# Attention scores on all 128 array rows: q of one head with zeros in the other head's rows, three products against k of both heads

## The chip, the cores and the metric

One Trainium2 chip, one of its cores, one launch. The metric is the device time of the program in microseconds (us): the median of three runs was 327.04 us (326.93 to 328.31).

## What is computed

A layer of a decoder for one sequence of 256 tokens and 1024 channels: norm, causal attention with 16 heads of 64, output projection, residual, norm, a feed-forward with a causal convolution of width 3 over its 2 x 2816 inner channels, residual, last norm. Since the sequence has only 256 tokens and the blocks of the reference's block-sparse attention are 256 long, the block choice falls away and plain causal attention is left:

```
hn = rmsnorm(x) * norm_mix;  q, k, v = split(hn @ w_qkv)          # 16 heads of 64
s = (q / 8) @ k.T;  s = where(k_pos <= q_pos, s, -1e30);  p = softmax(s)
x = x + (p @ v) @ w_o
hn = rmsnorm(x) * norm_ffn;  u = conv3(hn @ ffn_w_up) + b;  gate, up = split(u)
x = x + (silu(gate) * up) @ ffn_w_down
out = rmsnorm(x) * norm_final
```

All of it is in 32-bit floats. The kernel gets near to that precision by splitting each operand into a high and a low part of the type fp32r and adding three products: high x high, high x low, low x high (`mm3`, L213 to L217: line L215 is high x high, L216 and L217 the other two).

## The kernel before, in words

Everything stays in SBUF but the weights, which stream in: a unit of weights is loaded by SP's queue, ScalarE (ACT) writes its high part (L158), VectorE (DVE) its low part (L161).

The heads go in pairs: pair j holds heads 2j and 2j+1, the first in partitions 0 to 63, the second in 64 to 127. For each pair TensorE (PE) makes qT and kT (128 channels x 256 tokens each, 24 products of 256 columns per projection, all with 128 x 128 weights); then the scores; ACT and DVE make the softmax; PE transposes the probabilities (L331) and multiplies them with V.

The queries are taken in two tiles of 128. The first 128 queries see only the first 128 keys, the second 128 see all 256. The steps that the change touches, per pair:

- `q_hi` (L259, ACT) and `q_lo` (L266, DVE) take q out of PSUM. For the first 128 queries q is copied as plain 32-bit floats (QF). For the second 128 a tile QS holds, for each head, the high part in that head's own 64 partitions and the low part in the other 64.
- `k_hi` (L274, ACT) writes, for each head, a tile KH with the high part of that head's k twice, in its own 64 partitions and in the other 64: four copies. `k_lo` (L281, DVE) writes the low part KL in two pieces of 64 partitions.
- `scores` (L286, PE): for each head one plain 32-bit product of 128 columns on 64 rows (L289); then for each head a product of QS with KH on all 128 rows (L291), which is q_hi k_hi + q_lo k_hi, and q_hi k_lo on 64 rows (L292). The profile's records show two records for each plain 32-bit product, so L289 has four per pair.
- `softmax_dve` (L297, DVE, L303) reads the scores with mask and takes the maxima.

What sets the order: a table written out by hand. `START` and `LAST` are the steps before and after the steady part; `SCHED` is one "tick", in which PE runs a projection of pair j, the transposes of pair j-2, the scores of pair j-1, the second projection, and P V. Every engine runs its own instructions in the order of this table; nothing is reordered by a scheduler. In a tick `OL`, `KH`, `QL`, `H0`, `KL` (the low part of the attention's output, the splits of k and q, and of the next weights) come first, then PE's `A`, `TR`, `SC`, ... DVE thus has OL, QL, KL in this order ahead of the scores. Loads are issued when a weight buffer comes free, which is when the low part of the unit in it is written.

After the eight pairs come the output projection, the residual and its transposes, and the feed-forward, eleven steps of two "up" projections and one "down" (L627 on). The gains of the last norm, gF, are loaded at L601 from ACT's queue.

Of the kernel before, what the change touches and what calls it, by code (L numbers as in the profile page):

```python
# [27 lines left out]
# The order in which the steps of the attention are issued; every engine runs its own in this order.  # L28
# Steps: Q, K, V = evacuation of a projection, H / L = high and low part of a split, SC = scores, MX = mask and
# maximum, E = exp, RC / N = normalisation, TR = transposes, T = split of the transposed, PV = times V, O = split  # L30
# of the output, A / B = projections, W = output projection. START: before the ticks, SCHED: a tick (steps marked 1
# belong to the tick before), LAST: after them ("-": left over from the last tick).
# [18 lines left out]
def hybrid_layer(ctx: ExitStack, tc: tile.TileContext, a):  # L51
# [40 lines left out]
    gF = cst.tile([P, D], F32, name="gF")  # L92
# [10 lines left out]
    # the activation tables, too, are loaded meanwhile  # L103
    act.activation(st[:, 31:32], neghalf[:, 0:1], AF.Exp)

    # PE clock warm-up while the first loads are under way
# [124 lines left out]
    # sum of squares -> 1/rms  # L231
# [7 lines left out]
    def bcast_R(c, alloc):  # L239
        # R[p, t] = st[t, c + t // 128] on all partitions  # L240
        rp = alloc()
        for t in range(2):
            dg = wk.tile([P, P], F32, name="dg")
            dve.tensor_scalar(dg, ident, st[:, c + t:c + t + 1], None, op0=ALU.mult)
            pe.matmul(rp[:, t * P:(t + 1) * P], ones, dg, start=True, stop=True)
        act.activation(R, rp[:, :S], AF.Copy)

    # ================= attention =================
# [5 lines left out]
    QF, QS, KF, KH, KL = {}, {}, {}, {}, {}  # L254
    rows = [slice(0, 64), slice(64, P)]

    # The second 128 queries' scores: a head's q_hi and q_lo lie one above the other (the second head's
    # lo above its hi) against k_hi twice, which is q_hi k_hi + q_lo k_hi in one pass; then q_hi k_lo.
    def q_hi(j):  # L259
        QF[j] = wk.tile([P, S], F32, name="QF", tag="y1")  # L260
        QS[j] = wk.tile([P, 2, P], F32R, name="QS", tag="y0")
        for h in range(2):
            act.activation(QS[j][rows[h], h, :], qps[j][rows[h], P:S], AF.Copy)
        act.activation(QF[j][:, 0:P], qps[j][:, 0:P], AF.Copy)

    def q_lo(j):  # L266
        for h in range(2):
            dve.tensor_sub(QS[j][rows[1 - h], h, :], qps[j][rows[h], P:S], f32(QS[j][rows[h], h, :]))
# [5 lines left out]
    def k_hi(j):  # L274
        KH[j] = [wk.tile([P, S], F32R, name=f"KH{h}", tag=("mh", "ml")[h], bufs=3) for h in range(2)]
        for h in range(2):
            act.activation(KH[j][h][rows[h], :], KF[j][rows[h], :], AF.Copy)
        for h in range(2):
            act.activation(KH[j][h][rows[1 - h], :], KF[j][rows[h], :], AF.Copy)

    def k_lo(j):  # L281
        KL[j] = wk.tile([P, S], F32R, name="KL", tag="KT")
        for h in range(2):
            dve.tensor_sub(KL[j][rows[h], :], KF[j][rows[h], :], f32(KH[j][h][rows[h], :]))

    def scores(j):  # L286
        SP[j] = [psS(0), psS(1)]
        for h in range(2):
            pe.matmul(SP[j][h][:, 0:P], QF[j][rows[h], 0:P], KF[j][rows[h], 0:P], start=True, stop=True)  # L289
        for h in range(2):  # L290
            pe.matmul(SP[j][h][:, P:P + S], QS[j][:, h, :], KH[j][h], start=True, stop=False)  # L291
            pe.matmul(SP[j][h][:, P:P + S], QS[j][rows[h], h, :], KL[j][rows[h], :], start=False, stop=True)  # L292
# [483 lines left out]
```

## Time and profile before

| | |
|---|---|
| median of three runs (lowest, highest) | 327.04 us (326.93, 328.31) |
| the profiled execution, span from first to last instruction | 325.3 us |
| PE busy | 313.4 us (96%), 2087 products |
| DVE busy | 244.9 us (75%) |
| ACT busy | 211.5 us (65%) |
| mean granted clock of TensorE | 0.993 |

The profiled execution is known by its span; what lies around it is the difference to a run's time, 1.7 us against the median. A product's busy time in the profile is longer than the distance to the next one, since products overlap: the pace is read from start to start.

### The profile page before, as it was taken

To read this page: it belongs to the slowest core of one execution; us is meant where nothing else is said; L and a number is where in the kernel's file an instruction comes from. 1 tells how busy PE (TensorE), PEld (TensorE's weight loads), DVE (VectorE), ACT (ScalarE), POOL (GpSimd) and SP (SyncE) were. 2 spreads that over 40 slices of the span, in tenths; PEclk is the share of its full clock that TensorE was granted. 3 is DMA by queue.
4 is the path that set the end of the run, shared out by engine and by line. 5 is a ranking of instruction groups with operands and counts; after the bars stand their busy time and mean duration, and the time that the engine had idled before them with its cause. 6 is when DMAs were issued, how large, how long until landed. Compare 5 with 4: busy or idle time off the path is not lost.

```text
span 325.3 us, 5446 instructions
## 1 busy us (share of the span) xinstructions
PE 313.4 (96%) x2087; PEld 283.3 (87%) x2087; DVE 244.9 (75%) x478; ACT 211.5 (65%) x397; POOL 4.7 (1%) x17
## 2 busy tenths in 40 slices
PE   8799999999999999999999999999999999999990
PEld 5688988887987888999999999999999999999970
DVE  3764898877898985489998777777777777774754
ACT  5775999877998954577776555556555565553342
POOL 1000000000000000000000000000000000000002
PEclk9999999999999999999999999999999999999997
DMA  6998333844123197418765555555555512110003
GB/s 168 379 413 345 133 129 131 322 148 176 66 82 114 43 351 317 141 55 319 287 236 195 193 196 193 195 193 192 178 183 175 184 61 64 66 64 2 1 1 129
DMA packets 12698, 55.50 MB, mean 171 GB/s; under 512 B 1408, under 2 KB 2304, under 8 KB 8960
## 3 DMA queue, kind: packets, MB, share of 16 engines
q1 hardware_dynamic: 12384, 54.37, 46.2%
q10 hardware_dynamic: 288, 0.79, 0.7%
q8 instruction: 16, 0.26, 0.3%
q14 instruction: 10, 0.08, 0.1%
HBM read 54.10 MB, written 1.05 MB: 170 GB/s over the span
## 4 chain that ended last, share of the span: by engine, by line
PE 93%; DMA 2%; SPq 1%; issue 1%; ACT 1%; DVE 1%; POOLq 0%; POOL 0%
PE psA L215 21%; PE psA L217 21%; PE psA L216 20%; PE psT L217 4%; PE psT L216 4%; PE psT L215 4%; PE psS L216 3%; PE psS L217 3%; PE psS L215 3%; DMA raw<-in_wqk 2%; PE psT L331 2%; PE psS L291 2%; PE psS L292 2%; PE psS L289 1%; PE psA L406 1%
## 5 line engine op out<-in xcount | busy, mean ns | idle before, releaser
L215 PE MATMUL psA<-XTh,whi 128*128 128x256 f32 x288 | 81.8, 284 | 0.0
L217 PE MATMUL psA<-XTh,wlo 128*128 128x256 f32 x288 | 81.7, 284 | 0.0
L216 PE MATMUL psA<-XTl,whi 128*128 128x256 f32 x288 | 81.4, 283 | 0.0
L161 DVE TENSOR_TENSOR wlo<-raw,whi 128x1024 fp32r<-128x1024 f32 (+2 forms) x52 | 56.6, 1094 | 9.1 <-ACT whi L158 8.9
L215 PEld LDWEIGHTS psA<-XTh,whi 128*128 128x128 f32 x288 | 54.4, 189 | 1.2
L610 ACT ACTIVATE y<-pad,head 128x256 f32<-128x256 f32 x44 | 25.9, 600 | 44.4 <-DVE pad L606 44.4
L216 PEld LDWEIGHTS psA<-XTl,whi 128*128 128x128 f32 x288 | 54.2, 188 | 0.4
L217 PEld LDWEIGHTS psA<-XTh,wlo 128*128 128x128 f32 x288 | 54.3, 189 | 0.0
L158 ACT ACTIVATE whi<-raw 128x1024 fp32r<-128x1024 f32 (+2 forms) x52 | 48.6, 950 | 4.2 <-DMA raw<-in_wqk 2.7
L606 DVE TENSOR_TENSOR pad<-psA,R 128x256 f32<-128x256 f32 x44 | 18.1, 420 | 38.2 <-PE psA L217 35.5
L615 DVE SCALAR_TENSOR_TENSOR y<-pad,head,y 128x256 f32<-128x256 f32 x88 | 37.0, 478 | 1.6 <-ACT y L610 1.5
L161 DVE TENSOR_TENSOR dlo<-rawd,dhi 128x1024 fp32r<-128x1024 f32 x29 | 35.3, 1216 | 0.2
L158 ACT ACTIVATE dhi<-rawd 128x1024 fp32r<-128x1024 f32 x29 | 30.2, 1048 | 2.2 <-PE psA L217 2.1
L217 PE MATMUL psA<-XTh,OTl 128*128 128x256 f32 x80 | 22.8, 285 | 0.0
L217 PE MATMUL psA<-XTh,Vl 128*128 128x256 f32 x80 | 22.7, 284 | 0.0
L216 PE MATMUL psA<-XTl,OTh 128*128 128x256 f32 x80 | 22.7, 284 | 0.0
L216 PE MATMUL psA<-XTl,Vh 128*128 128x256 f32 x80 | 22.7, 283 | 0.0
L215 PE MATMUL psA<-XTh,Vh 128*128 128x256 f32 x80 | 22.5, 281 | 0.0
L215 PE MATMUL psA<-XTh,OTh 128*128 128x256 f32 x80 | 22.5, 281 | 0.0
L657 ACT ACTIVATE sact<-y 128x256 f32<-128x256 f32 x22 | 9.2, 418 | 16.4 <-DVE y L615 16.4
L217 PE MATMUL psT<-dhi,ml 128*128 128x512 f32 x42 | 16.7, 396 | 0.0
L216 PE MATMUL psT<-dlo,mh 128*128 128x512 f32 x42 | 16.6, 395 | 0.0
(169 smaller groups left out, 663.2 us busy)
## 6 DMA issues: line engine op xcount, KB each, us to landing
raw<-in_wup SPq DMA_DIRECT2D x22, 1024.0 KB, 4.8
rawd<-in_wdn SPq DMA_DIRECT2D x22, 512.0 KB, 3.5
raw<-in_wqk SPq DMA_DIRECT2D x5, 1024.0 KB, 9.3
rawd<-in_wo SPq DMA_DIRECT2D x8, 512.0 KB, 3.9
raw<-in_wv SPq DMA_DIRECT2D x4, 512.0 KB, 6.7
raw<-in_wv SPq DMA_DIRECT2D x2, 1024.0 KB, 4.7
raw<-in_wqk SPq DMA_DIRECT2D x6, 256.0 KB, 6.3
x_sb<-in_x SPq DMA_DIRECT2D x2, 512.0 KB, 9.3
```

Of the source, the lines that this page charges most:

```text
L158: act.activation(self.hi[:, c], self.raw[:, c], AF.Copy)
L161: dve.tensor_sub(self.lo[:, c], self.raw[:, c], f32(self.hi[:, c]))
L215: pe.matmul(out, lh, rh, start=first, stop=False)
L216: pe.matmul(out, lh, rl, start=False, stop=False)
L217: pe.matmul(out, ll, rh, start=False, stop=last)
L291: pe.matmul(SP[j][h][:, P:P + S], QS[j][:, h, :], KH[j][h], start=True, stop=False)
L292: pe.matmul(SP[j][h][:, P:P + S], QS[j][rows[h], h, :], KL[j][rows[h], :], start=False, stop=True)
L331: pe.transpose(PT[j][:, h, b * P:(b + 1) * P], PR[j][:, h, b * P:(b + 1) * P], ident)
L606: dve.tensor_mul(pads[c % 2][g][:, 2:S + 2], gps[c, g][:, :S], R)
L610: act.activation(y[c, g], pads[c % 2][g][:, 2:S + 2], AF.Identity, scale=cw[:, 2, g * NC + c:g * NC + c + 1], bias=cb[:, g * NC + c:g * NC ...
L615: dve.scalar_tensor_tensor(y[c, g], pads[c % 2][g][:, j:j + S], cw[:, j, col:col + 1], y[c, g], op0=ALU.mult, op1=ALU.add)
L657: act.activation(sact, y[c, 0], AF.Silu)
```

## The change

q is kept in four constant tiles, QMh and QMl (high and low), two of each for odd and even pairs, 128 x 2 x 256. For head h only its own 64 partitions are ever written by `q_hi` and `q_lo`; the other 64 are set to zero once, by eight memsets on POOL at the start. k is split like any other operand: one high tile of 128 x 256, one low tile, with both heads in it. The scores are `mm3` on all 128 rows for each head and each tile of queries: the rows of the other head meet zeros. That is 12 products per pair, six of 128 columns (first queries) and six of 256 columns, in the place of two plain 32-bit ones and four fp32r ones.

To make room, gF is no longer a constant tile but two halves that take the buffers of the probabilities (tag PR), loaded in two transfers at the same place; the small diagonal tile of `bcast_R` takes the buffer y0.

```
+    QMh = [cst.tile([P, 2, S], F32R, name=f"QMh{i}") for i in range(2)]
+    QMl = [cst.tile([P, 2, S], F32R, name=f"QMl{i}") for i in range(2)]
+    for i in range(2):
+        for t in (QMh[i], QMl[i]):
+            pool.memset(f32(t[64:P, 0, :]), 0.0)
+            pool.memset(f32(t[0:64, 1, :]), 0.0)
...
     def q_hi(j):
-        QF[j] = wk.tile([P, S], F32, name="QF", tag="y1")
-        QS[j] = wk.tile([P, 2, P], F32R, name="QS", tag="y0")
         for h in range(2):
-            act.activation(QS[j][rows[h], h, :], qps[j][rows[h], P:S], AF.Copy)
-        act.activation(QF[j][:, 0:P], qps[j][:, 0:P], AF.Copy)
+            act.activation(QMh[j % 2][rows[h], h, :], qps[j][rows[h], :S], AF.Copy)
 
     def q_lo(j):
         for h in range(2):
-            dve.tensor_sub(QS[j][rows[1 - h], h, :], qps[j][rows[h], P:S], f32(QS[j][rows[h], h, :]))
+            dve.tensor_sub(QMl[j % 2][rows[h], h, :], qps[j][rows[h], :S], f32(QMh[j % 2][rows[h], h, :]))
...
     def k_hi(j):
-        KH[j] = [wk.tile([P, S], F32R, name=f"KH{h}", tag=("mh", "ml")[h], bufs=3) for h in range(2)]
-        for h in range(2):
-            act.activation(KH[j][h][rows[h], :], KF[j][rows[h], :], AF.Copy)
-        for h in range(2):
-            act.activation(KH[j][h][rows[1 - h], :], KF[j][rows[h], :], AF.Copy)
+        KH[j] = wk.tile([P, S], F32R, name="KH", tag="mh", bufs=3)
+        act.activation(KH[j], KF[j], AF.Copy)
 
     def k_lo(j):
-        KL[j] = wk.tile([P, S], F32R, name="KL", tag="KT")
-        for h in range(2):
-            dve.tensor_sub(KL[j][rows[h], :], KF[j][rows[h], :], f32(KH[j][h][rows[h], :]))
+        KL[j] = wk.tile([P, S], F32R, name="KL", tag="ml", bufs=3)
+        dve.tensor_sub(KL[j], KF[j], f32(KH[j]))
 
     def scores(j):
         SP[j] = [psS(0), psS(1)]
+        qh, ql = QMh[j % 2], QMl[j % 2]
         for h in range(2):
-            pe.matmul(SP[j][h][:, 0:P], QF[j][rows[h], 0:P], KF[j][rows[h], 0:P], start=True, stop=True)
-        for h in range(2):
-            pe.matmul(SP[j][h][:, P:P + S], QS[j][:, h, :], KH[j][h], start=True, stop=False)
-            pe.matmul(SP[j][h][:, P:P + S], QS[j][rows[h], h, :], KL[j][rows[h], :], start=False, stop=True)
+            for t in range(2):
+                q, n = slice(t * P, (t + 1) * P), (t + 1) * P
+                o = SP[j][h][:, 0:P] if t == 0 else SP[j][h][:, P:P + S]
+                mm3(o, (qh[:, h, q], ql[:, h, q]), (KH[j][:, :n], KL[j][:, :n]), True, True)
...
-    nc.scalar.dma_start(gF, bass.AP(tensor=a["gF"].tensor, offset=a["gF"].offset, ap=[[0, P], [1, D]]))
+    gF = [wk.tile([P, 512], F32, name=f"gF{i}", tag="PR") for i in range(2)]
+    for i in range(2):
+        nc.scalar.dma_start(gF[i], bass.AP(tensor=a["gF"].tensor, offset=a["gF"].offset + 512 * i, ap=[[0, P], [1, 512]]))
```

On PE, the scores of a pair in the steady part; psS are the two score tiles, one per head (left out<-moving operand, stationary operand, with the size of the output). Before:

```order
L289 MATMUL psS_655<-KF,QF 128x128
L289 MATMUL psS_656<-KF,QF 128x128
L291 MATMUL psS_655<-KH_607,QS 128x256
L292 MATMUL psS_655<-KL,QS 128x256
L291 MATMUL psS_656<-KH_608,QS 128x256
L292 MATMUL psS_656<-KL,QS 128x256
```

With the change (L222 to L224 are now the three lines of `mm3`):

```order
L222 MATMUL psS_651<-KH,QMh_90 128x128
L223 MATMUL psS_651<-KL,QMh_90 128x128
L224 MATMUL psS_651<-KH,QMl_92 128x128
L222 MATMUL psS_651<-KH,QMh_90 128x256
L223 MATMUL psS_651<-KL,QMh_90 128x256
L224 MATMUL psS_651<-KH,QMl_92 128x256
L222 MATMUL psS_652<-KH,QMh_90 128x128
L223 MATMUL psS_652<-KL,QMh_90 128x128
L224 MATMUL psS_652<-KH,QMl_92 128x128
L222 MATMUL psS_652<-KH,QMh_90 128x256
L223 MATMUL psS_652<-KL,QMh_90 128x256
L224 MATMUL psS_652<-KH,QMl_92 128x256
```

Six products became twelve, head by head, and k's low part (KL) is read by the second product instead of the fourth.

On DVE, between two softmaxes of the steady part (OTl is the low part of the attention's output, QS and QM that of q, KL that of k, wlo that of the next weights). Before:

```order
L272 TENSOR_TENSOR KF<-psA,R 128x256
L325 TENSOR_SCALAR PR<-PR,sm 128x256 x2
L359 TENSOR_TENSOR OTl<-psA,OTh 64x256 x2
L268 TENSOR_TENSOR QS<-psA,QS 64x128 x2
L284 TENSOR_TENSOR KL<-KF,KH_607 64x256
L284 TENSOR_TENSOR KL<-KF,KH_608 64x256
L161 TENSOR_TENSOR wlo<-raw,whi 128x1024
```

With the change:

```order
L275 TENSOR_TENSOR KF<-psA,R 128x256
L325 TENSOR_SCALAR PR<-PR,sm 128x256 x2
L359 TENSOR_TENSOR OTl<-psA,OTh 64x256 x2
L271 TENSOR_TENSOR QMl_93<-psA,QMh_91 64x256 x2
L283 TENSOR_TENSOR KL<-KF,KH 128x256
L168 TENSOR_TENSOR wlo<-raw,whi 128x1024
```

The places are the same; q's low part is twice as wide, k's is one instruction instead of two.

## Rows read from the trace of the kernel before

**Rows 1.** The page: the span, and each engine's busy time.
```profile
span 325.3 us, 5446 instructions
PE 313.4 (96%) x2087; PEld 283.3 (87%) x2087; DVE 244.9 (75%) x478; ACT 211.5 (65%) x397; POOL 4.7 (1%) x17
```

**Rows 2.** The chain that ended last, by line, shares of the span.
```profile
PE psA L215 21%; PE psA L217 21%; PE psA L216 20%; PE psT L217 4%; PE psT L216 4%; PE psT L215 4%; PE psS L216 3%; PE psS L217 3%; PE psS L215 3%; DMA raw<-in_wqk 2%; PE psT L331 2%; PE psS L291 2%; PE psS L292 2%; PE psS L289 1%; PE psA L406 1%
```

**Rows 3.** Timeline of PE, scores of pair 0: start, duration (us), engine, line, operands.
```profile
33.22 0.28 PE L215 MATMUL psA<-XTh,whi 128*128 128x256 f32 x1
...
34.16 0.28 PE L217 MATMUL psA<-XTh,wlo 128*128 128x256 f32 x1
34.38 0.49 PE L289 MATMUL psS<-KF,QF 64*128 64x128 f32 x4
34.80 0.39 PE L291 MATMUL psS<-KH,QS 128*128 128x256 f32 x1
35.11 0.38 PE L292 MATMUL psS<-KL,QS 64*128 64x256 f32 x1
...
36.05 0.39 PE L215 MATMUL psA<-XTh,whi 128*128 128x256 f32 x1
36.27 0.27 PE L216 MATMUL psA<-XTl,whi 128*128 128x256 f32 x1
```

**Rows 4.** Timeline of PE's weight loads, same stretch.
```profile
33.46 0.19 PEld L215 LDWEIGHTS psA<-XTh,whi 128*128 128x128 f32 x1
...
35.11 0.18 PEld L292 LDWEIGHTS psS<-KL,QS 64*128 64x128 f32 x1
```

**Rows 5.** Timeline of PE, scores of pair 1, first record and second one behind them.
```profile
42.59 0.49 PE L289 MATMUL psS<-KF,QF 64*128 64x128 f32 x4
...
44.49 0.28 PE L216 MATMUL psA<-XTl,whi 128*128 128x256 f32 x1
```

**Rows 6.** The chain in order of time: start, length, what.
```profile
28.29 0.45 PE psS L245 x4
...
42.01 0.66 PE psT L331 x6
```

**Rows 7.** Timeline of PE before the scores of pair 4: products of 512 columns.
```profile
71.71 0.40 PE L215 MATMUL psA<-whi,XTh 128*128 128x512 f32 x1
71.94 0.39 PE L216 MATMUL psA<-wlo,XTh 128*128 128x512 f32 x1
...
73.15 0.49 PE L289 MATMUL psS<-KF,QF 64*128 64x128 f32 x4
```

**Rows 8.** Groups by line and form, ACT, DVE and POOL: busy us, mean ns.
```profile
L279 ACT ACTIVATE KH<-KF 64x256 fp32r<-64x256 f32 x16 | 6.7, 417 | 0.4
L665 ACT ACTIVATE mh<-m 128x256 fp32r<-128x256 f32 x22 | 9.2, 418 | 11.3 <-DVE m L662 11.3
L284 DVE TENSOR_TENSOR KL<-KF,KH 64x256 fp32r<-64x256 f32 x16 | 6.7, 419 | 0.5
L668 DVE TENSOR_TENSOR ml<-m,mh 128x256 fp32r<-128x256 f32 x22 | 9.2, 418 | 1.5 <-ACT mh L665 1.5
L268 DVE TENSOR_TENSOR QS<-psA,QS 64x128 fp32r<-64x128 f32 x16 | 4.6, 289 | 1.7 <-ACT QF L264 1.4
L359 DVE TENSOR_TENSOR OTl<-psA,OTh 64x256 fp32r<-64x256 f32 x12 | 5.0, 420 | 1.4 <-ACT OTh L354 1.2
L82 POOL MEMSET mask<- 128x256 f32 x1 | 0.3, 312 | 0.0
```

**Rows 9.** Timeline of DVE before the scores of pair 0.
```profile
30.78 0.59 DVE L268 TENSOR_TENSOR QS<-psA,QS 64x128 fp32r<-64x128 f32 x2
...
32.91 1.41 DVE L376 SCALAR_TENSOR_TENSOR Vl<-psT,st,Vh 128x512 fp32r<-128x512 f32 x2
34.24 0.86 DVE L284 TENSOR_TENSOR KL<-KF,KH 64x256 fp32r<-64x256 f32 x2
```

**Rows 10.** Timeline of DVE before the scores of pair 4.
```profile
71.20 0.85 DVE L359 TENSOR_TENSOR OTl<-psA,OTh 64x256 fp32r<-64x256 f32 x2
72.06 0.59 DVE L268 TENSOR_TENSOR QS<-psA,QS 64x128 fp32r<-64x128 f32 x2
```

**Rows 11.** Windows: stretch, length, then busy us (count) of PE, PEld, DVE, ACT, POOL; clock, DMA.
```profile
51.93:61.20 9.27, 9.27 (x70) 8.34 (x70) 7.93 (x21) 8.29 (x23) 0.00 (x0) 1.00 0.34 123
...
140.00:313.00 173.00, 173.00 (x1217) 162.50 (x1217) 133.39 (x232) 99.71 (x146) 0.00 (x0) 1.00 0.42 150
```

More of the change, by code (lines that the diff above doesn't have):

```diff
@@ L90, in hybrid_layer @@
             pool.memset(pads[i][g][:, 0:2], 0.0)
-    gF = cst.tile([P, D], F32, name="gF")
+    QMh = [cst.tile([P, 2, S], F32R, name=f"QMh{i}") for i in range(2)]
[4 more added lines that the diff above has]
+            pool.memset(f32(t[0:64, 1, :]), 0.0)
     x_sb = cst.tile([P, 2, D], F32, name="x_sb")
@@ L242, in bcast_R @@
         for t in range(2):
-            dg = wk.tile([P, P], F32, name="dg")
+            dg = wk.tile([P, P], F32, name="dg", tag="y0")
             dve.tensor_scalar(dg, ident, st[:, c + t:c + t + 1], None, op0=ALU.mult)
@@ L253, in hybrid_layer @@
     qps, kps, SP, PR, PT, OP = {}, {}, {}, {}, {}, {}
-    QF, QS, KF, KH, KL = {}, {}, {}, {}, {}
+    KF, KH, KL = {}, {}, {}
     rows = [slice(0, 64), slice(64, P)]
     def q_hi(j):
-        QF[j] = wk.tile([P, S], F32, name="QF", tag="y1")
-        QS[j] = wk.tile([P, 2, P], F32R, name="QS", tag="y0")
         for h in range(2):
-            act.activation(QS[j][rows[h], h, :], qps[j][rows[h], P:S], AF.Copy)
-        act.activation(QF[j][:, 0:P], qps[j][:, 0:P], AF.Copy)
+            act.activation(QMh[j % 2][rows[h], h, :], qps[j][rows[h], :S], AF.Copy)
     def q_lo(j):
         for h in range(2):
-            dve.tensor_sub(QS[j][rows[1 - h], h, :], qps[j][rows[h], P:S], f32(QS[j][rows[h], h, :]))
+            dve.tensor_sub(QMl[j % 2][rows[h], h, :], qps[j][rows[h], :S], f32(QMh[j % 2][rows[h], h, :]))
     def k_evac(j):
@@ L693, in gains @@
         hs = slice(512 * half, 512 * half + 512)
-        dve.tensor_mul(x_sb[:, t, hs], x1[:, t, hs], gF[:, hs])
+        dve.tensor_mul(x_sb[:, t, hs], x1[:, t, hs], gF[half])
     def scaled(t, half):
@@ L734, in hybrid_layer @@
             nc.scalar.dma_start(a["out"][P:, :512], x_sb[:, 1, :512])
-        dve.scalar_tensor_tensor(x_sb[:, t, 512:], x1[:, t, 512:], st[:, 14 + t:15 + t], gF[:, 512:],
+        dve.scalar_tensor_tensor(x_sb[:, t, 512:], x1[:, t, 512:], st[:, 14 + t:15 + t], gF[1],
                                  op0=ALU.mult, op1=ALU.mult)
```

## The prediction

> **What bounds the kernel now.** I read the busy times first: TensorE (PE) is busy in 313.4 of 325.3 us, DVE in 244.9, ACT in 211.5 [rows 1]. That alone is a weak sign, since a busy PE may be a slow one, so the chain of waits comes next: it lies on PE almost throughout, and what other engines add is the load of the first weights at the start and the last norm at the end [rows 2]. The windows say the same by stage: in a tick of the attention PE fills 9.27 of 9.27 us while DVE has 7.93 and ACT 8.29, and in the feed-forward it fills 173.00 of 173.00 [rows 11]. So a microsecond taken from PE between 20 and 313 us comes off the end, as long as ACT and DVE keep up; work taken from ACT or DVE alone is worth nothing.
>
> Then I read PE's pace, from start to start. Nine projection products of 256 columns begin at 33.22 and the ninth at 34.16: 0.94 us / 8 = 0.118 us each [rows 3]. The score block beside them has another pace: the four L289 records take 0.42 us, and then L291 to L292 takes 0.31, though L291 has the same 256 columns and the same 128 rows as a projection. The loads tell why: in the projections the load of 0.19 us lies under earlier products (one every 0.118 us); in the block the load of L292 starts at 35.11, with its own product [rows 3, 4]. Where a product on 128 rows follows one on 64 rows or the other way round, nothing is loaded ahead. The first projection behind the block pays it too: 36.05 to 36.27 is 0.22 instead of 0.118.
>
> **The change, part by part.**
>
> *What goes.* For pair 1 the block runs from 42.59 to the second projection product behind it at 44.49: 1.90 us, less 0.118 for the projection between = 1.78 us [rows 5]. The blocks of the other pairs look alike. Pair 0 begins 0.22 us behind the last projection, so it has 0.10 us of switch in front as well [rows 3].
>
> *What comes.* Twelve products on 128 rows, in one mode with all their neighbours, so I take no switch. Six have 256 columns: 6 x 0.118 = 0.708 us. Six have 128 columns in fp32r, and **no row shows such a product**. Bounds: below, the step from 512 columns (71.71 to 71.94, 0.23 us [rows 7]) to 256 (0.118) is proportional, which would make 128 columns 0.06. Above, a plain 32-bit product of 128 columns on 128 rows, L245: four records in 0.45 us are two products, 0.225 each [rows 6]. Between them stand the transposes, 128 columns on 128 rows with a 128 x 128 load each, six in 0.66 us = 0.110 [rows 6]. I take 0.110: it is the nearest in shape, and a load of 0.19 us has to be fitted in for every product, which is already paced at 0.118 for twice the columns. Block: 0.708 + 0.66 = 1.37 us; it saves 1.78 - 1.37 = 0.41 us.
>
> The Trainium skill ("TensorE: Matmul & The Clock Gate", Back-to-back issue gap) gives about 81 ns per product for a stream of loads and products of 128 columns. By it the block would take 1.19 us and the sum would end near 323.0 us; no run here shows that pace for 32-bit operands.
>
> The same page (Part 3) has a rule against this change: a weight load overlaps products in flight only when it goes to another row group. This trace differs: in the projections all rows are the same and the load does overlap [rows 3, 4].
>
> *k's low part is read earlier.* Before, the fourth product needed it, now the second. Pair 0: DVE runs without a gap from 30.78 [rows 9]; the two low parts of q grow from 0.59 to about 0.85 (2 x 64x128 at 289 ns become 2 x 64x256 like L359 at 420 [rows 8]), so KL starts at 34.24 + 0.26 = 34.50 and, as one instruction of 0.42 [L668 in rows 8], ends at 34.92. The second product could start at 34.28 + 0.11 = 34.39 and waits 0.53. Eleven products follow, 5 x 0.110 + 6 x 0.118 = 1.26, up to 36.18. The old block ended, with its delayed projection, at 36.27 - 0.118 = 36.15. **Pair 0 gains nothing.** Pair 4: the low part of the output ends at 72.05 [rows 10], + 0.85 + 0.42 = 73.32; the second product would start at 73.15 + 0.11 = 73.26 [rows 7] and waits 0.06: gain 0.35. For the other six I take no wait: each tick DVE has 2 x (420 - 289) more for q and 2 x 419 - 418 less for k, 0.16 us less in all, and ACT four copies of k fewer (two of 417 ns as L279, two like them) for one of 418: 1.25 us less [rows 8]; its copies of q go from three narrow ones to two of 256 columns. That lets the next weights' high part, which DVE needs for the low part, start earlier. With PE's tick at 8.86 instead of 9.27, DVE's 7.8 and ACT's 7.0 still fit [rows 11].
>
> *At nothing:* the eight memsets on POOL, each half the size of L82's 312 ns [rows 8], so at most 2.5 us at the very start; the first product that reads the zeros is that of pair 0's scores at 34 us [rows 3]. Without that cover PE would wait for POOL, 2.5 us at most, once. The second transfer of gF costs one more issue on ACT ahead of the feed-forward, where ACT is busy 99.71 of 173 us [rows 11]; its bytes are the same and read only at the end.
>
> *Sum:* six pairs x 0.41 = 2.5, pair 4 0.35, pair 0 nothing: 2.8 us off. The profiled execution has a span of 325.3 us; the median of the runs, 327.04, lies 1.7 above it, and I take the sum from the median: **324.2 us**. With 0.100 to 0.118 for the short product and 0.3 us either way for the waits, its own range is 323.4 to 325.1.
>
> **The rivals.**
>
> *Short fp32r products run like plain 32-bit ones (slower).* The place is the first-queries half of every block, six products each; the price is 0.225 [rows 6]. Block 0.708 + 1.35 = 2.06, 0.28 longer than before. Six pairs 1.7, pair 4 0.28 (the first product now covers the wait), pair 0: 34.92 + 5 x 0.225 + 6 x 0.118 = 36.75 against 36.15, 0.6. In all 2.6 us slower: **329.6**. It decides from 0.178 us on per short product, where 6 x that + 0.708 reaches 1.78. For it: the kernel's only products of 128 columns that multiply are the plain ones, so nothing here shows fp32r at this width at the full pace. Against it: an fp32r product has one record and a plain one two, and the transposes of the same width need only 0.110.
>
> *Paced by columns alone:* 0.061 each, block 1.07, 0.29 more gained in seven pairs and 0.25 in pair 0: 5.1 us off, **321.9**. Against it: a load of 0.19 us for each.
>
> *k's low part comes late everywhere,* as in pair 0, and PE waits in each block for what it saved: **327.0**, no change. For it: DVE is busy 86% of a tick, and the second product is a tight place. Against it: DVE and ACT have less to do.
>
> *No load overlaps on the same rows* (the rule of Part 3 above): 12 x 0.31 = 3.72, 1.94 more per pair, 342.5; the projections' 0.118 speaks against it.
>
> **How the numbers follow.** A measurement of this kernel can tell about 0.5%, 1.6 us, from no change. Forecast 0.50, short products slow 0.27, columns alone 0.10, late everywhere 0.10, no overlap 0.03. Faster by over 0.5%: 0.50 + 0.10 = 0.60; within: 0.10; slower: 0.27 + 0.03 = 0.30. The range holds the forecast, its upper neighbours and the slow short products: 322.8 (a short product at about 0.08) to 329.9. It leaves out columns alone and no overlap. The likeliest case by itself has 323.4 to 325.1.
>
> **What would show it.** In the profile after, twelve score products per pair; from start to start 0.118 for the wide ones, 0.110 for the short ones; no step of 0.31 and no 0.22 behind the block; a wait of half a microsecond before the second product of pair 0 alone, for DVE; ACT's busy time down by about 10 us in the attention. Wrong: short products 0.2 us apart; a PE idle on DVE's KL in each tick; a step of 0.2 or more at the edges of the block although all rows are used.

## The result, and the profile after

| | before | after |
|---|---|---|
| median of 13 runs each, us (lowest, highest) | 327.04 (326.21, 329.86) | 325.18 (323.33, 326.10) |
| the profiled execution, us | 325.3 span | 324.20, of it 322.5 span |
| mean granted clock of TensorE | 0.993 | 0.992 |

The ratio of after to before is 0.9932, with 0.9911 to 0.9953 as its interval: about 2.2 us faster (1.5 to 2.9), 0.7%. The forecast was 324.2, a saving of 2.8 us; its direction holds. The time lies in the wide range (322.8 to 329.9), which also holds a kernel made slower, and just above the range of the likeliest case (323.4 to 325.1). The profile shows that this nearness has two errors in it that partly cancel: PE saved more per pair than forecast, and waits took back more.

The page of after, busy times and the chain by line, answers to [rows 1, 2]:

```profile
span 322.5 us, 5483 instructions
PE 311.4 (97%) x2119; PEld 285.7 (89%) x2119; DVE 243.4 (75%) x470; ACT 203.2 (63%) x365; POOL 7.2 (2%) x25
...
PE psA L223 19%; PE psA L224 19%; PE psA L222 19%; PE psS L223 4%; PE psS L224 4%; PE psS L222 4%; PE psT L224 4%; PE psT L223 4%; PE psT L222 4%; DMA raw<-in_wqk 1%; PE psT L331 1%; DVE wlo L168 1%; PE psA L406 1%; PE psA L410 1%; PE psA L408 1%
```

PE has 32 product records more (the chain is still on it), ACT is busy 8.3 us less, DVE 1.5 less. The window of a tick (stretch, length, then PE, PEld, DVE, ACT, POOL) answers to [rows 11]:

```profile
50.73:59.50 8.77, 8.77 (x76) 8.63 (x74) 7.70 (x21) 7.22 (x18) 0.00 (x0) 1.00 0.37 122
```

A steady tick takes 8.77 us in the place of 9.27 and PE still fills it. It gives 0.50, not 0.41. Where that comes from shows in PE's timeline of pair 1 (start, duration), which answers to [rows 5]:

```profile
41.38 0.82 PE L331 MATMUL psT<-ident,PR 128*128 128x128 f32 x6
41.95 0.30 PE L222 MATMUL psS<-KH,QMh 128*128 128x128 f32 x1
42.09 0.28 PE L223 MATMUL psS<-KL,QMh 128*128 128x128 f32 x1
42.21 0.28 PE L224 MATMUL psS<-KH,QMl 128*128 128x128 f32 x1
42.32 0.33 PE L222 MATMUL psS<-KH,QMh 128*128 128x256 f32 x1
42.49 0.28 PE L223 MATMUL psS<-KL,QMh 128*128 128x256 f32 x1
...
42.72 0.22 PE L222 MATMUL psS<-KH,QMh 128*128 128x128 f32 x1
42.78 0.27 PE L223 MATMUL psS<-KL,QMh 128*128 128x128 f32 x1
...
43.41 0.28 PE L222 MATMUL psA<-XTh,whi 128*128 128x256 f32 x1
43.53 0.28 PE L223 MATMUL psA<-XTl,whi 128*128 128x256 f32 x1
```

From the first score product to the second projection product it is 1.58 us; before it was 1.90: 0.32 saved. The other 0.17 lies in front of the block: from the transposes L331 to the first score product it is 0.57 us now, and was 0.74, from this row of PE's timeline of the kernel before to its 42.59 [rows 5]:

```profile
41.85 0.82 PE L331 MATMUL psT<-ident,PR 128*128 128x128 f32 x6
```

The trace of before had that switch in it. In its timeline of PE's weight loads, the first load of the block is held 0.17 us for nothing that the profile can name (the list of waits has this seven times, 1.4 us in all):

```profile
42.59 0.30 PEld L289 LDWEIGHTS psS<-KF,QF 64*128 64x128 f32 x4 [0.17 <-issue]
```

The same timeline of after shows the pace of the block now:

```profile
41.92 0.19 PEld L222 LDWEIGHTS psS<-KH,QMh 128*128 128x128 f32 x1
42.03 0.19 PEld L223 LDWEIGHTS psS<-KL,QMh 128*128 128x128 f32 x1
...
42.26 0.19 PEld L222 LDWEIGHTS psS<-KH,QMh 128*128 128x128 f32 x1
42.37 0.19 PEld L223 LDWEIGHTS psS<-KL,QMh 128*128 128x128 f32 x1
...
43.30 0.19 PEld L222 LDWEIGHTS psA<-XTh,whi 128*128 128x128 f32 x1
```

Twelve loads in 1.38 us, one every 0.115, whatever the width of the product behind them. The products' own steps of 0.06 to 0.17 only shift within that pace: a product starts 0.06 us behind the start of its load where it follows a short one (42.26 to 42.32) and 0.12 where it follows a wide one (42.37 to 42.49). So the step from a wide product to the next is long where the lag grows, and the one from a short product to the next is short where it shrinks (42.72 to 42.78).

**What was lost again.** PE's waits for DVE's low parts (total us, times, longest), of which before had none in PE's ticks:

```profile
PEld psS L223 <- DVE KL L283: 0.9, 3, 0.4
PEld psA L223 <- DVE dlo L168: 0.7, 2, 0.4
...
PE psS L223 <- DVE KL L283: 0.2, 1, 0.2
```

KL is k's low part; dlo is the low part of the output projection's weights. (One more load, ahead of pair 0, waits 0.2 us for the low part of other weights.) Between the starts of the eight score blocks and up to the first transpose of the residual (L549, 123.87 us before, 121.39 after) PE's timeline gives these intervals:

| from pair to pair | 0 to 1 | 1 to 2 | 2 to 3 | 3 to 4 | 4 to 5 | 5 to 6 | 6 to 7 | 7 to L549 | sum |
|---|---|---|---|---|---|---|---|---|---|
| before, us | 8.21 | 9.27 | 9.27 | 12.02 | 12.00 | 9.27 | 8.57 | 20.88 | 89.49 |
| after, us | 7.98 | 8.78 | 8.77 | 11.50 | 11.89 | 8.78 | 8.75 | 20.97 | 87.42 |
| saved, us | 0.23 | 0.49 | 0.50 | 0.52 | 0.11 | 0.49 | -0.18 | -0.09 | 2.07 |

Pairs 0, 4 and 6 wait for KL in their own block, and the last two intervals hold waits for dlo or late steps of the output projection (two waits for dlo, at 117.16 and 119.42 us, cost 0.45 together; two steps of 0.35 and 0.31 in the place of 0.23 before pair 7's scores, whose loads wait for nothing that is named, cost 0.20). Of the profiled runs' difference of 2.8 us this stretch gives 2.07; 0.41 is the start, where pair 0's scores begin anywhere from 33.5 to 36.0 us in the runs below, and the rest the end. So below I compare the *stretch*, pair 0's first score product to L549, which leaves the start out: 89.49 before, 87.42 after. Each stretch is that of one execution; TensorE's granted clock is 1.00 in it in every run here.

Pair 6 in DVE's timeline, q's and k's low parts:

```profile
90.82 0.86 DVE L271 TENSOR_TENSOR QMl<-psA,QMh 64x256 fp32r<-64x256 f32 x2
91.71 0.43 DVE L283 TENSOR_TENSOR KL<-KF,KH 128x256 fp32r<-128x256 f32 x1
```

and in PE's, the first two score products:

```profile
91.67 0.30 PE L222 MATMUL psS<-KH,QMh 128*128 128x128 f32 x1
92.19 0.33 PE L223 MATMUL psS<-KL,QMh 128*128 128x128 f32 x1 [0.22 <-DVE KL L283]
```

The second product starts 0.05 us after KL ends (91.71 + 0.43), and KL stands behind the two instructions of q's low part.

Both low parts hang on more than DVE's own work. In pair 4 two low parts of weights, the low parts of the output and of q, and KL follow one another on DVE without a gap, and before the first of them DVE waits 1.69 us for the weights' high part (DVE's timeline of after):

```profile
66.94 2.36 DVE L168 TENSOR_TENSOR wlo<-raw,whi 128x1024 fp32r<-128x1024 f32 x2 [1.69 <-ACT whi L165]
```

dlo is late by way of a weight load. DVE, without a gap from 103.09 on, is done with the unit in the weight buffer at 108.18, SP issues the next load into it at 108.25, and ACT can take the high part only at 113.10, after this wait (total us, times, longest):

```profile
ACT dhi L165 <- DMA rawd<-in_wo: 1.8, 1, 1.8
```

Then DVE, idle for 1.47 us, goes on, and dlo is written from 115.88 to 117.10, 0.06 us before PE's load at 117.16. Before, ACT waited for no such load at this place.

In the groups by line and form (count, busy us and mean ns) these answer to [rows 8]:

```profile
L271 DVE TENSOR_TENSOR QMl<-psA,QMh 64x256 fp32r<-64x256 f32 x16 | 6.7, 421 | 0.2
...
L283 DVE TENSOR_TENSOR KL<-KF,KH 128x256 fp32r<-128x256 f32 x8 | 3.4, 425 | 0.2
...
L279 ACT ACTIVATE KH<-KF 128x256 fp32r<-128x256 f32 x8 | 3.3, 414 | 0.1
```

Each operation costs what the forecast took: q's low part 421 ns a piece, twice a pair, KL 425 and k's high part 414, once.

### The profile page after: what moved, and what is told of

Read it like the earlier page. It is cut to its first block, busy times and chain, and to the rows that moved or that the text cites. A ratio compares the mean times of both kernels' runs of the same rounds, so it can differ in the third digit from the quotient of the medians.

```text
span 322.5 us, 5483 instructions
## 1 busy us (share of the span) xinstructions
PE 311.4 (97%) x2119; PEld 285.7 (89%) x2119; DVE 243.4 (75%) x470; ACT 203.2 (63%) x365; POOL 7.2 (2%) x25
## 4 chain that ended last, share of the span: by engine, by line
PE 87%; DVE 4%; ACT 3%; issue 2%; DMA 1%; SPq 1%; POOLq 0%; POOL 0%; DVEq 0%
PE psA L223 19%; PE psA L224 19%; PE psA L222 19%; PE psS L223 4%; PE psS L224 4%; PE psS L222 4%; PE psT L224 4%; PE psT L223 4%; PE psT L222 4%; DMA raw<-in_wqk 1%; PE psT L331 1%; DVE wlo L168 1%; PE psA L406 1%; PE psA L410 1%; PE psA L408 1%
## 5 line engine op out<-in xcount | busy, mean ns | idle before, releaser
L224 PE MATMUL psA<-XTh,wlo 128*128 128x256 f32 x288 | 81.7, 284 | 0.0
L222 PE MATMUL psA<-XTh,whi 128*128 128x256 f32 x288 | 81.2, 282 | 0.0
L222 PEld LDWEIGHTS psA<-XTh,whi 128*128 128x128 f32 x288 | 54.5, 189 | 0.4
L224 PEld LDWEIGHTS psA<-XTh,wlo 128*128 128x128 f32 x288 | 54.3, 189 | 0.2 <-DVE wlo L168 0.2
L224 PE MATMUL psA<-XTh,OTl 128*128 128x256 f32 x80 | 22.8, 285 | 0.0
L224 PE MATMUL psA<-XTh,Vl 128*128 128x256 f32 x80 | 22.7, 284 | 0.0
L222 PE MATMUL psA<-XTh,Vh 128*128 128x256 f32 x80 | 22.5, 281 | 0.0
L222 PE MATMUL psA<-XTh,OTh 128*128 128x256 f32 x80 | 22.5, 281 | 0.0
L313 ACT ACTIVATE PR<-PR,mx 128x128 f32<-128x128 f32 (+1 forms) x32 | 14.4, 450 | 4.0 <-DVE mx L303 3.9
L224 PE MATMUL psT<-dhi,ml 128*128 128x512 f32 x42 | 16.7, 396 | 0.0
```

What stands on the lines that cost most here:

```text
L222: pe.matmul(out, lh, rh, start=first, stop=False)
L224: pe.matmul(out, ll, rh, start=False, stop=last)
L313: act.activation(PR[j][:, h, c], PR[j][:, h, c], AF.Exp, scale=-1.0, bias=mx[j][:, i:i + 1], accum_out=sm[j][:, i:i + 1])
```

## The experiments

Two questions: what on PE the saving comes from, and what the waits come from. In most expectations A is by and large the prediction's account and B a rival. Medians are of several runs, ratios are to the kernel before on the same chip (its medians there: 327.81 for e1, e2, e4, e5; 326.57 for e3, e6, e7, e8; 326.69 for e9, e10).

This table sets PE's part beside the outcome. The second column is pair 1 in PE's timeline, from the start of the transposes to the second product of the projection behind the block. The third is eight times the difference to before, a rough promise if all pairs were alike. The fourth is what the stretch really lost.

| kernel | pair 1, us | promise, us | stretch shorter by, us | median, us | ratio (interval) |
|---|---|---|---|---|---|
| before | 2.64 | | | 327.04 | |
| after | 2.15 | 3.9 | 2.07 | 325.18 | 0.9932 (0.9911, 0.9953) |
| e10, room and zeros alone | 2.64 | 0.0 | 0.06 | 326.37 | 0.9990 (0.9966, 1.0014) |
| e6, before with zeros in KL | 1.87 | 6.2 | 3.71 | 323.48 | 0.9907 (0.9876, 0.9938) |
| e1, 64 rows, head by head | 2.14 | 4.0 | 3.42 | 324.69 | 0.9915 (0.9882, 0.9948) |
| e8, 64 rows, heads in turn | 1.85 | 6.3 | 6.22 | 320.57 | 0.9828 (0.9801, 0.9855) |
| e2, KL read last | 2.16 | 3.8 | 1.76 | 324.56 | 0.9935 (0.9907, 0.9963) |
| e4, copies back on ACT | 2.15 | 3.9 | 0.82 | 326.24 | 0.9978 (0.9953, 1.0004) |
| e3, scaling on ACT | 2.15 | 3.9 | -0.57 | 327.49 | 1.0039 (1.0017, 1.0062) |
| e9, scaling on POOL | 2.14 | 4.0 | 2.52 | 324.04 | 0.9916 (0.9884, 0.9948) |
| e5, plain first queries | 1.92 | 5.8 | 5.04 | 321.97 | 0.9847 (0.9818, 0.9876) |
| e7, two products | 1.69 | 7.6 | 1.52 | 325.42 | 0.9954 (0.9932, 0.9977) |

### e10: the side edits alone

Before, with gF in two halves in the buffers of the probabilities and eight memsets on POOL of tiles that nothing reads (each as long as in the change). The move of `bcast_R`'s small tile is left out.

```
+    QMh = [cst.tile([P, 2, P], F32R, name=f"QMh{i}") for i in range(2)]
+    QMl = [cst.tile([P, 2, P], F32R, name=f"QMl{i}") for i in range(2)]
+    for i in range(2):
+        for t in (QMh[i], QMl[i]):
+            pool.memset(f32(t[64:P, :, :]), 0.0)
+            pool.memset(f32(t[0:64, :, :]), 0.0)
...
+    gF = [wk.tile([P, 512], F32, name=f"gF{i}", tag="PR") for i in range(2)]
```

> The kernel before with what the change does around the scores alone: gains of the last norm in two halves in the buffers of the probabilities, two transfers, and memsets of four q tiles on GpSimd at the start, which nobody reads; the scores are those of before. Theory A (these cost nothing): the time of the kernel before within 0.5 us. Theory B (the second transfer's issue on ScalarE or GpSimd's start shows): 0.5 to 1.5 us slower, and the score changes are worth that much more.

Measured: 326.37 us (325.65 to 328.22), ratio 0.999 with 1 in its interval; the stretch is 89.43 us against 89.49. The memsets and the second transfer cost nothing that can be seen.

### e6: the switch alone

Before, with one thing changed on PE: KL has zeros in the other head's rows, so that L292 runs on 128 rows (L295 here). POOL sets the zeros once, and gF makes room as in e10.

```
+            dve.tensor_sub(KLp[j % 2][h][rows[h], :], KF[j][rows[h], :], f32(KH[j][h][rows[h], :]))
...
-            pe.matmul(SP[j][h][:, P:P + S], QS[j][rows[h], h, :], KL[j][rows[h], :], start=False, stop=True)
+            pe.matmul(SP[j][h][:, P:P + S], QS[j][:, h, :], KLp[j % 2][h], start=False, stop=True)
```

> The kernel before with one part changed: k's low part lies in a tile per head with zeros in the other head's rows, so that the product q_hi k_lo runs on all 128 rows like the one before it. The number of products, the plain ones on 64 rows and the copies of k stay. Theory A (each change between 64 and 128 rows costs 0.2 us in the block): of the changes only the one into the plain products and the one out of them stay; the last three products and the projection behind them come down from 0.31 to about 0.118 each, 0.7 us per pair, 5.6 us at most; some of it lost to late low parts: 321.5 to 323.5. Theory B (the slow steps belong to the operands, as the product of the stacked q with the doubled k, not to the change of rows): 326.5 to 327.5.

Measured: 323.48 us (322.06 to 324.6). PE's timeline of pair 1:

```profile
44.03 0.49 PE L292 MATMUL psS<-KF,QF 64*128 64x128 f32 x4
44.45 0.38 PE L294 MATMUL psS<-KH,QS 128*128 128x256 f32 x1
44.68 0.28 PE L295 MATMUL psS<-KLp,QS 128*128 128x256 f32 x1
44.80 0.28 PE L294 MATMUL psS<-KH,QS 128*128 128x256 f32 x1
44.92 0.28 PE L295 MATMUL psS<-KLp,QS 128*128 128x256 f32 x1
45.03 0.28 PE L219 MATMUL psA<-XTh,whi 128*128 128x256 f32 x1
```

The wide ones, 0.31 apart in [rows 3], are now 0.12 apart with the same columns and the same operands otherwise; the change of rows behind L292 remains and costs 0.23 instead of 0.118, once. That is the mechanism by itself. It also beats the change on PE (1.87 against 2.15), with half its products, yet its stretch falls only 3.71 us where 6.2 are promised: waits appear in PE's queue for low parts of the probabilities (0.8 us) and weights (0.5), and for ACT's k copies (0.7).

### e1 and e8: 64 rows without zeros

In e1 the twelve products run on the head's own 64 rows, in the order of the change. The zeros are written but not read.

```
-                mm3(o, (qh[:, h, q], ql[:, h, q]), (KH[j][:, :n], KL[j][:, :n]), True, True)
+                mm3(o, (qh[r, h, q], ql[r, h, q]), (KH[j][r, :n], KL[j][r, :n]), True, True)
```

> The changed kernel, but each of the twelve score products runs only on its head's 64 rows (the zeros aren't multiplied); everything else stays. Theory A (the time lies in the changes between 64 and 128 rows, where no weight load runs ahead): inside the block nothing changes its row count, so the products stand about 0.11 us apart as in the changed kernel, and only the entry, the change of head and the exit cost some 0.1 to 0.2 us each: about 0.4 us per pair, 3 us in all, near 328. Theory B (a product on 64 rows is slow by itself, 0.31 us as L292 was): twelve steps of 0.31, 3.7 us per block against 1.4, some 18 us in all, 343.

Measured: 324.69 us (323.32 to 324.86), near neither figure of the expectation: both had the two heads' products one after the other. PE's timeline of pair 1:

```profile
43.02 0.82 PE L332 MATMUL psT<-ident,PR 128*128 128x128 f32 x6
43.77 0.33 PE L222 MATMUL psS<-KH,QMh 64*128 64x128 f32 x1
...
44.44 0.33 PE L222 MATMUL psS<-KH,QMh 64*128 64x256 f32 x1
44.45 0.28 PE L224 MATMUL psS<-KH,QMl 64*128 64x256 f32 x1
...
44.94 0.38 PE L222 MATMUL psA<-XTh,whi 128*128 128x256 f32 x1
45.16 0.28 PE L223 MATMUL psA<-XTl,whi 128*128 128x256 f32 x1
```

The switches are back at both edges (0.75 in front, 0.22 behind), but the twelve products take 1.17 us instead of 1.46. At 44.44 and 44.45 two wide products start 0.01 us apart: the first of one head and the last of the other, on different row halves. On one half such products are 0.11 apart or more. The halves do not even keep the program's order: the second head's first product starts at 44.05, the first head's first wide one, which the program issues earlier, at 44.16.

That suggested e8: take the heads in turn, so that every product has its partner beside it. q then needs no zeros: one tile each for the high and low part, one instruction each on ACT and DVE for both heads.

```
-                mm3(o, (qh[:, h, q], ql[:, h, q]), (KH[j][:, :n], KL[j][:, :n]), True, True)
+            for l, r, i in ((qh, KH[j], 0), (ql, KH[j], 1), (qh, KL[j], 2)):
+                for h in range(2):
+                    o = SP[j][h][:, 0:P] if t == 0 else SP[j][h][:, P:P + S]
+                    pe.matmul(o, l[rows[h], q], r[rows[h], :n], start=i == 0, stop=i == 2)
...
-            dve.tensor_sub(QMl[j % 2][rows[h], h, :], qps[j][rows[h], :S], f32(QMh[j % 2][rows[h], h, :]))
+        dve.tensor_sub(QL[j % 2], qps[j][:, :S], f32(QH[j % 2]))
```

> No zeros at all: q and k are split like any other operand, one high and one low tile for both heads, written by one instruction each; three fp32r products per head on the head's own 64 rows, the two heads in turn. In the variant on 64 rows head by head, products of the second head ran beside those of the first. Theory A (products on different halves of the rows run side by side): the block is three steps of 0.11 and three of 0.118 for both heads, 0.7 us against 1.46, with about 0.4 us for the changes at its edges: some 0.4 us less per pair than in the changed kernel, and VectorE has 0.4 us less per tick, so its waits go: 320 to 321.5. Theory B (they only seemed to run side by side): twelve steps of 0.11 to 0.118, 1.4 us and the changes: 326 or more, less what VectorE's relief gives, 325.

Measured: 320.57 us (320.07 to 322.18), 1.7% under before (2.0 to 1.5), the lowest time here, though its interval overlaps that of e5. PE's timeline of pair 1:

```profile
43.43 0.33 PE L287 MATMUL psS<-KH,QH 64*128 64x128 f32 x2
43.60 0.27 PE L287 MATMUL psS<-KH,QL 64*128 64x128 f32 x2
...
44.31 0.38 PE L218 MATMUL psA<-XTh,whi 128*128 128x256 f32 x1
44.54 0.28 PE L219 MATMUL psA<-XTl,whi 128*128 128x256 f32 x1
```

Two products fill the 0.33 or 0.27 us that one had filled, and the twelve take 0.88 us. Both edges still pay the switch. PE's promise and the stretch agree here (6.3 and 6.22), and no wait of PE for a low part is listed: DVE's q low part is one instruction of 0.42 us a pair instead of two.

### e2: k's low part read later

For each tile of queries, high x high of both heads first, then q's low part, then KL, which the fifth product is the first to need.

```
+            for h in range(2):
+                pe.matmul(o[h], qh[:, h, q], KH[j][:, :n], start=True, stop=False)
+            for h in range(2):
+                pe.matmul(o[h], ql[:, h, q], KH[j][:, :n], start=False, stop=False)
+            for h in range(2):
+                pe.matmul(o[h], qh[:, h, q], KL[j][:, :n], start=False, stop=True)
```

> The changed kernel with the same twelve products in another order: for each tile of queries first high x high of both heads, then q low x k high, then q high x k low, so that k's low part is read by the fifth product instead of the second, some 0.3 us later. Theory A (PE waits for k's low part in a few pairs and loses 1 us of what the score blocks save): the waits of PE for KL, 1.1 us in four places of the profile, go, and the time falls by 0.7 to 1.1 us against the changed kernel, to about 324.2. Theory B (DVE is late anyway, and PE waits a little later for the next low part): 325.2, as the changed kernel.

Measured: 324.56 us (323.58 to 327.17), the same as after by its interval; the stretch is 87.73 us, not shorter. The waits for KL fall from 1.1 to 0.3 us, and this one of PE's loads takes their place (0.7 in after):

```profile
PEld psA L223 <- DVE dlo L168: 1.5, 2, 1.1
```

A PE that does not stop for KL stops for dlo. Here too dlo hangs on the load: DVE gives the buffer free at 108.04, hardly earlier than in after, and ACT waits 2.5 us for the load, where it waited 1.8.

### e4, e3, e9: load put on ACT, moved to ACT, taken off DVE

e4 gives ACT three copies of k per pair that nothing reads, about what the change took away:

```
+        for h in range(3):
+            act.activation(dup[rows[h % 2], :], KF[j][rows[1 - h % 2], :], AF.Copy)
```

> The changed kernel with three more copies of k per pair on ScalarE, into a tile that nobody reads: ScalarE has as many copies of k per pair as before the change. Theory A (the gain is PE's alone; ScalarE's relief is worth nothing or little): 325.2 to 325.7, PE's pace in the score blocks as in the changed kernel. Theory B (a good part of the gain comes from ScalarE, whose earlier high parts let VectorE and PE go on): 326.3 to 327.0, with waits of PE on high or low parts of weights.

Measured: 326.24 us (325.32 to 329.09). With the same products on PE the stretch is 1.25 us longer than after's. Waits of PE's loads and of PE itself for KL are 1.3 and 0.6 us, for dlo 1.3 and 0.5. The median lies below theory B's figures, and its interval touches both after's and no change, so the stretch and the waits are the firmer evidence.

e3 moves the scaling of the second queries' probabilities from DVE to ACT:

```
-                dve.tensor_scalar(PR[j][:, h, P:P + S], PR[j][:, h, P:P + S], r, None, op0=ALU.mult)
+            act.activation(PR[j][:, h, c], PR[j][:, h, c], AF.Copy, scale=r)
```

> The changed kernel with the scaling of the second queries' probabilities (two instructions of 346 ns per pair) taken from VectorE and given to ScalarE. Theory A (what the changed kernel loses is VectorE's lateness: PE's waits for the low parts of k and of the output projection's weights, 1.1 + 0.7 us in the profile): VectorE has 0.6 us less per tick, the waits go, about 1.5 us faster than the changed kernel's 325.2: 323.7. Theory B (VectorE only hands on the lateness of ScalarE's high parts): ScalarE has about 1 us more per tick, the waits stay or grow, 325.2 to 326.5, as with the added copies.

Measured: 327.49 us (327.06 to 329.2), by 0.4% slower than before. DVE was relieved (239.3 us busy, 4.1 less than after), yet KL and dlo came later still (1.9 and 1.9 us in the loads' waits): DVE's low parts need ACT's high parts, and ACT had become the late one (209.0 us busy, 5.8 more; DVE waits 5.8 us for the high part of the attention's output, 2.7 in after). ACT's wait for the load ahead of dlo is 2.7 us.

e9 moves the same scaling to POOL, which is idle then, and so loads neither:

```
-                dve.tensor_scalar(PR[j][:, h, P:P + S], PR[j][:, h, P:P + S], r, None, op0=ALU.mult)
+                pool.tensor_scalar(PR[j][:, h, P:P + S], PR[j][:, h, P:P + S], r, None, op0=ALU.mult)
```

> The changed kernel with the scaling of the second queries' probabilities (two instructions of 346 ns per pair on VectorE) given to GpSimd (POOL), which has nothing to do in the attention. Given to ScalarE it cost 2 us, since the waits of PE grew. Theory A (VectorE's and ScalarE's sum of work in the ticks makes k's low part and the weights' low parts late, so relief of either one counts): VectorE has 0.6 us less per tick and nobody has more, the waits of PE for k's low part and the output projection's low parts (1.1 + 0.7 us in the changed kernel's profile) go: 323.4 to 324. Theory B (what is late is late for another reason, such as the order of the table or GpSimd's own time before the transposes): 325 to 326.5.

Measured: 324.04 us (323.74 to 325.67), the stretch 86.97, 0.45 us shorter than after's. The wait for dlo is gone; this one stays:

```profile
PEld psS L223 <- DVE KL L283: 1.0, 3, 0.4
```

So the two waits differ. dlo was late because DVE had too much to do, by way of the weight load: relieved, DVE gives the buffer free at 107.52, the load is issued at 107.58 in the place of 108.25, and ACT no longer waits for it. KL does not move, since DVE's relief comes ahead of a wait for ACT and only makes that wait longer. In pair 4 it is 2.21 us in the place of 1.69 (in pair 6 0.68 in the place of 0.16), and behind it KL's chain is the same:

```profile
67.04 2.36 DVE L168 TENSOR_TENSOR wlo<-raw,whi 128x1024 fp32r<-128x1024 f32 x2 [2.21 <-ACT whi L165]
```

The gain against after is near what two kernels' medians can be told apart by; the vanished line is the firmer evidence.

### e5 and e7: fewer products on all rows

e5 computes the first queries as one plain 32-bit product per head, again on 128 rows with zeros; q's high and low parts are then needed for the second queries alone, half as wide.

```
+            pe.matmul(SP[j][h][:, 0:P], QFp[j % 2][:, h, :], KF[j][:, 0:P], start=True, stop=True)
+        for h in range(2):
+            mm3(SP[j][h][:, P:P + S], (QMh[j % 2][:, h, :], QMl[j % 2][:, h, :]), (KH[j], KL[j]), True, True)
```

> The changed kernel with the first 128 queries' scores as one plain 32-bit product per head, on all 128 rows with zeros, in the place of three fp32r products. The three take 0.06 + 0.11 + 0.11 us in the changed kernel's profile, and the wide one behind them 0.17 instead of 0.118: 0.33 per head. Theory A (a plain product costs 0.225 as L245 shows it): 0.1 less per head, 0.2 per pair, 1.7 us in all, and a little less for VectorE's low parts: 323.3. Theory B (a change between plain and fp32r products costs as one of rows does): nothing gained or up to 1.5 us lost, 325 to 326.7.

Measured: 321.97 us (321.31 to 323.46). PE's timeline of pair 1:

```profile
42.09 0.61 PE L291 MATMUL psS<-KF,QFp 128*128 128x128 f32 x4
42.45 0.36 PE L223 MATMUL psS<-KH,QMh 128*128 128x256 f32 x1
...
43.24 0.28 PE L223 MATMUL psA<-XTh,whi 128*128 128x256 f32 x1
```

That is under both theories' figures. By the products' starts the first queries take 0.36 us, where six short fp32r products take 0.66, and the block 1.15. But the first plain record starts 0.11 behind its load and the fp32r product behind them 0.03, so the loads are the fairer count:

```profile
41.98 0.53 PEld L291 LDWEIGHTS psS<-KF,QFp 128*128 128x128 f32 x4
42.43 0.19 PEld L223 LDWEIGHTS psS<-KH,QMh 128*128 128x128 f32 x1
```

Four loads take 0.45 us, 0.11 each, and two make a plain product, near the 0.225 that the expectation took from L245. The whole pair is 0.23 us shorter than after's (1.92 against 2.15): ten loads in the place of twelve. No wait for KL or dlo is left: KL is needed 0.57 us into the block (at 42.66), and q's low part costs DVE less.

e7 goes further on PE: plain first queries, and two products per head for the second ones, with k's high part in one half of the rows and its low part in the other. That needs two more copies of q on ACT than e5.

```
+            pe.matmul(SP[j][h][:, P:P + S], Q2[j % 2][:, h, :], KH[j][h], start=True, stop=False)
+            pe.matmul(SP[j][h][:, P:P + S], Q1[j][:, h, :], KH[j][h], start=False, stop=True)
```

> All on 128 rows with fewer products: the first queries' scores are one plain 32-bit product per head with zeros in the other head's rows; the second queries' are two fp32r products per head against one tile that holds k's high part in the head's own rows and its low part in the other ones: q high in both halves, then q low with zeros. ScalarE writes k's high part twice and q's high part four times, VectorE has the work of the kernel before. Theory A (PE's time in the block and VectorE's low parts decide): plain products 0.36, then four of 0.12 to 0.17, about 0.92 us against 1.27 with three products for the second queries; VectorE and ScalarE are loaded as in the kernel before and the ticks are shorter, so some waits: 319.5 to 321.5. Theory B (the copies and low parts bound the ticks): not faster than the variant with one plain product, 322 or more.

Measured: 325.42 us (323.62 to 326.5). The pair is the shortest of all, 0.46 us under after's with eight loads in the place of twelve (the block is 0.92, 41.20 to 42.12), and the kernel no better than the change: its loads wait 2.5 us for k's tile, in all eight pairs, and 1.6 us for the probabilities' low part. Of 7.6 us promised on PE the stretch gives 1.52.

## Why the prediction was right, and where not

**The mechanism: right.** The steps of 0.31 and 0.22 that the prediction read in [rows 3] are gone, and e6 removes them by changing rows alone. That the side edits cost nothing was right (e10).

**Short products of 0.110: right, to the digit by luck.** Their loads come every 0.115, near the pace that the forecast took from the transposes, which have a load each. (Their 0.66 us in [rows 6] is a piece of the chain and not six steps, but by their starts they are 0.11 apart as well.) Six short steps of pair 1 are 0.14, 0.12, 0.11, 0.06, 0.12 and 0.11, 0.66 us in all, the forecast's 0.66; how the block divides into short and wide steps hangs on the lag between load and product, and "Six have 256 columns: 6 x 0.118 = 0.708" came out at 0.80, with a step of 0.17 behind each first wide product. The block is 1.46 us, not 1.37. The rival with 0.225 needs blocks longer than before, and no step is that long. "Paced by columns alone" is out too: the step of 0.06 occurs once in this block, and the loads keep 0.115.

**"Pair 0 begins 0.22 us behind the last projection, so it has 0.10 us of switch in front as well": mis-sized.** A switch in front is in every pair, 0.17 us behind transposes (pairs 1 to 6) and about 0.1 in pairs 0 and 7. Adding it, a steady pair saves 0.32 + 0.17 = 0.49 and not 0.41. The profile of before had the row (the load held 0.17 "issue"); I had read the step behind the block and not the one ahead of it.

**"For the other six I take no wait": failed.** Of the six, pair 6 waits for KL, and the output projection is late before and behind pair 7. In pair 6 the second product starts 0.52 us behind the first, where pair 1 has 0.14: 0.38 lost. The forecast for the two pairs that it did look at was off as well. Pair 4, with 0.06, lost 0.31 (71.00 to 71.45); 0.17 of that is the switch in front: with it gone the block begins 2.15 us earlier than before (71.00 against 73.15), the low part of the output ahead of KL only 1.98 (69.22 against 71.20). Pair 0, for which "nothing" was forecast with a wait of 0.53, waits 0.28 and gains 0.06 (the rest of its 0.23 in the table is the switch in front of pair 1). For the six the prediction counted DVE's time per tick (0.16 us less), which is an average; what decides is when KL ends against the moment at which PE reads it. KL ends some 0.17 us earlier (0.26 more for q, 0.43 less for k), but PE reads it 0.14 us into the block, where it was 0.74 (42.59 to 43.33 in the timeline of before). The trace of before had the sign for pair 6: its KL ends at 94.73, 0.31 us into the block that begins at 94.42, nearly as late as pair 4's 0.40 (DVE's timeline of before):

```profile
93.86 0.87 DVE L284 TENSOR_TENSOR KL<-KF,KH 64x256 fp32r<-64x256 f32 x2
```

DVE's 7.70 of 8.77 us look like room, and are not at that place; in pair 4 the idle time lies ahead of KL's chain, in a wait for ACT.

**"Work taken from ACT or DVE alone is worth nothing": not true of the changed kernel.** For the kernel before no run tried it; PE has no wait for them in its ticks there. Once PE is faster, ACT's relief is part of the gain: given back in e4, it costs 1.25 us of the stretch. e3 shows the other side, ACT loaded and everything late. The busy time of ACT fell by 8.3 us, where "about 10" was forecast.

**Sum.** Eight pairs at 0.49 are 3.9 us; the stretch gives 2.07. The forecast's 2.8 lies between, from a saving too small and a loss too small. The rival "k's low part comes late everywhere" was put at 0.10: in the profile it is true in three pairs of eight, and the late steps of the output projection add 0.65. Counted place by place it closes: 0.32 to 0.36 in and behind eight blocks, 0.17 in front of six and 0.09 in front of pair 7 make 3.7, and the 1.62 lost at the places named leave 2.1. That the sum came near the time is thus luck in part.

**The rule against the change.** The Trainium skill ("TensorE: Matmul & The Clock Gate", Part 3: Packing small matmuls) says that a weight load overlaps products in flight only if it goes to another row group. The block of after differs: all rows are the same, and a load of 0.19 us starts every 0.115 us.

What stays open: how e6's shortfall (6.2 promised, 3.71 found) divides among its waits, whether the pace of 0.115 belongs to the loads or to the products (each product here has its own load), and whether KL moved ahead of q's low part on DVE would help the change; that order was not tried.

## What to carry to other kernels

Read a change of array rows at both of its edges, in the loads' timeline: here it cost 0.17 us in front and 0.1 behind each block, and 0.2 at each product where rows alternated. When PE gets faster, price the waits by the end time of each operand against the moment of its first use, pair by pair, and follow a late operand back past the engine that writes it, to the high part or the load that this engine waited for; a mean busy share of 86% hid three waits. And before padding with zeros, try the two row halves as partners: the same products without zeros took 0.88 us instead of 1.46 (1.85 instead of 2.15 with the switches at both edges) and cost the other engines less. The trace of before had a sign of it, in the plain products (below).

## What the runs showed of the hardware

- **Row halves run side by side.** fp32r products on rows 0 to 63 and on rows 64 to 127 overlap (e1) and start together when they are neighbours (e8: two in 0.33 us). The Trainium skill says this ("TensorEngine Tiling (Array Packing)", Key Properties): tiles run loads and products in parallel, and a change of the tiling mode drains the engine. The trace agrees with both: e8's pairs, and its edges, 0.74 from the transposes to the first score product (42.69 to 43.43; 0.57 in after) and 0.23 behind the block (0.12 in after). The plain 32-bit products of the kernel before did the same: the two heads' first records, 0.37 us each, fill 0.38 together, and the other two start at 42.81. Yet no time is gained by it here: the four take 0.43 us with the switch behind them (42.59 to 43.02), four on all rows 0.45 by their loads (e5).

```profile
42.59 0.38 PE L289 MATMUL psS<-KF,QF 64*128 64x128 f32 x2
```

- **Narrow products on all rows go at the pace of their loads.** One 128 x 128 load every 0.115 us, for 128 as for 256 columns, and every 0.11 for the plain ones of e5: by pair, twelve, ten and eight loads make 2.15, 1.92 and 1.69 us (after, e5, e7).
- **POOL is slow at scaling.** The instruction that DVE does in 347 ns takes it 1394 ns on average, here in e9's groups; moving it could help only because POOL is idle there:

```profile
L325 POOL TENSOR_SCALAR PR<-PR,sm 128x256 f32<-128x256 f32 x16 | 22.2, 1394 | 61.3 <-DVE sm L317 61.3
```
